# One core, a two-layer hybrid mixer scheduled by its own planner: GpSimd's products and sums may go to VectorE, and the planner counts the SBUF port that the two share

## The chip, the cores and the metric

The kernel runs on one core of a Trainium2 chip. The core has five engines that work side by side, each through its own instructions in order: TensorE (PE; its weight loads are listed apart as PEld), VectorE (DVE), ScalarE (ACT), GpSimd (POOL), and SyncE (SP), which here only issues transfers. An instruction waits at the head of its engine's queue until the semaphores that it names are set, and everything behind it on that engine waits too. The metric is the device time of one execution in microseconds (us); lower is better.

## The reference

Two layers (`DEPTH = 2`) over 256 context tokens and 512 latent tokens of width 1024. One projection `w_in` feeds three branches, which are merged by gates and projected by `w_out`.

```python
def _ssd_chunked(xdt, adt, bm, cm, s0):                 # 32 heads of 64, states of 128
    def body(state, xs):
        xc, ac, bc, cc = xs
        cum = jnp.cumsum(ac, axis=1)
        seg = cum[:, :, None] - cum[:, None, :]
        lmat = jnp.exp(jnp.where(mask, seg, -jnp.inf))
        cb = jnp.einsum('btgn,bsgn->btsg', cc, bc)
        y = jnp.einsum('btsgh,bsghp->btghp', cb[..., None] * lmat, xc)
        y = y + jnp.einsum('btgn,bghnp->btghp', cc, state) * jnp.exp(cum)[..., None]
        dec = jnp.exp(cum[:, -1:] - cum)
        state = state * jnp.exp(cum[:, -1])[..., None, None] \
            + jnp.einsum('bsgn,bsghp->bghnp', bc, xc * dec[..., None])
        return state, y
...
def _lru_gates(xa, wr, br, wi, bi, lam):
    ...
    a = jnp.exp(log_a)
    b = jnp.sqrt(-jnp.expm1(2.0 * log_a)) * (i * xa).astype(jnp.float32)
    return a, b                                         # then h_t = a_t h_{t-1} + b_t
...
def _finish(s, ya, yb, yc, xs, p):
    pa = (ya * jax.nn.silu(s[1])) @ p['w_pa']           # recurrence (LRU)
    ob = _rmsnorm(yb, p['gla_norm_g']).reshape(bn, length, GLA_DV) * jax.nn.silu(s[5])
    pb = ob @ p['w_pb']                                 # gated linear attention (GLA)
    ...
    pc = oc.reshape(bn, length, SSD_INNER) @ p['w_pc']  # state-space branch (SSD)
    g = jax.nn.sigmoid(s[10]).reshape(bn, length, N_BRANCH, D_MODEL)
    merged = g[:, :, 0] * pa + g[:, :, 1] * pb + g[:, :, 2] * pc
    return merged @ p['w_out']
```

All three branches run in both directions. The context's last states start the latent scans.

## The kernel before

Everything is fp32. A product with weights is made of three matmuls of split operands: a weight tile `raw` of 128x1024 arrives by DMA, half of it at a time is cast to `wh` (on ACT or DVE, L328 or L329), and DVE subtracts to get the rest, `wl` (L343). PE then adds `wh` by high input, `wh` by low input and `wl` by high input into a PSUM tile `pp`. The four buffers of `wh` and of `wl` come free as PE finishes with them.

A layer runs in stages. In the **SSD stage** (four groups of two quarters) PE works through weight matmuls while short chains of other work are woven in, in PSUM tiles `aux`:
- the state chain, `ssd_update`: `xw` = `xt` times a decay (POOL), cast to `xwh` (ACT or DVE), remainder `xwl` (DVE or POOL), three matmuls with `btok`, then `sb` or `sf` (the backward and forward states) = old state times decay (POOL) plus the PSUM result (DVE);
- the mask chain, `ssd_ms`: `rr` from DRAM, biases on ACT, a predicated copy with `mlt` (DVE, L388), exp (ACT), times `cb` (POOL, 128x512), a predicated copy with `kd` (DVE), then eight matmuls `aux<-rr,xt`;
- the outputs, `ssd_scan`: `ec` = PSUM times `ec` (DVE), the sum of its two halves (POOL), plus PSUM (DVE), then `gz` times `ec` (DVE); at a group's end `ssd_finish` sums four squares `r<-r,r` (POOL), normalises, and splits `gz` into `oh` and `ol`.

The **GLA stage** follows, then the **LRU stage** (eight blocks: `lru_rec` squares `av` into `w` on POOL, 128x768, and DVE takes `w` times `th`, two gates and three scans), then the output stage.

A planner written in Python, `Sched.loop`, sets the order of all of it while the program is built. Many streams of work are open at once; each shows its next operation. The planner knows a cost for each (`vcost`, `acost`, `gcost`), when each engine and each tile comes free by these costs, and takes the operation that can start first. An operation with more than one way (`any_op`) takes the engine on which it would end first. `copy`, `affine` and `sub` have two ways; `tt`, which makes nearly all of POOL's products and sums, has one, named by its `pool` argument. The result is a fixed order for each engine. What the costs miss shows on the chip as waits.

Of the kernel before, what the change touches and what calls it, by code (L numbers as in the profile page):

```python
# [14 lines left out]
PSUM = bass.MemoryType.PSUM  # L15
# [53 lines left out]
class Cell:  # L69
# [3 lines left out]
    def __init__(self, w=0.0):  # L73
        self.w, self.we, self.r, self.re, self.slots = w, None, 0.0, None, None
# [66 lines left out]
class Sched:  # L141
# [6 lines left out]
    def __init__(self):  # L148
        self.streams = []
        self.done = set()  # L150
        self.cells = {}
        self.eng_free = {"PE": 0.0, "DVE": 0.0, "ACT": 0.0, "POOL": 0.0, "SP": 0.0}
        self.dma_free = 0.0
        self.warm_up = HAM_WINDOW
        self.act_set = None
        self.seq = 0
        self.now = 0.0
# [26 lines left out]
                r = c.r + slack  # L184
        return r

    def op(self, eng, outs, ins, cost, emit):
        yield from self.any_op([(eng, cost, emit)], outs, ins)

    def any_op(self, ways, outs, ins):  # L190

        outs = [self.cell(o) for o in outs]
        ins = [self.cell(i) for i in ins if i is not None and not isinstance(i, (int, float))]
        yield ("op", ways, outs, ins)
        eng, cost, emit = ways[self.way]
        start = self.start_of(eng, outs, ins)
        if eng == "PE":
            if start - self.eng_free[eng] > HAM_WINDOW:
                self.warm_up = HAM_WINDOW
            if self.warm_up > 0:  # L200
                cost *= 2
                self.warm_up -= cost
        extra = emit()
        if isinstance(extra, int):
            cost += extra
        if eng == "SP":
            self.eng_free[eng] = start + 470
            self.dma_free = max(start, self.dma_free) + cost
            fin = self.dma_free + 3000
        else:  # L210
            fin = self.eng_free[eng] = start + cost
        self.now = max(self.now, start)
        for c in outs:
            if fin > c.w:
                c.w, c.we = fin, eng
        for c in ins:
            if fin > c.r:
                c.r, c.re = fin, eng
# [23 lines left out]
    def loop(self):  # L242
        while self.streams:
            best = None
            for s in list(self.streams):
                while s in self.streams:
                    c = s.cur
                    if c is None or (c[0] == "need" and all(n in self.done for n in c[1])) \
                            or (c[0] == "slots" and len(c[1].free) >= c[2]):
                        self.advance(s)  # L250
                        continue
                    break
                else:
                    continue
                if c[0] == "op":
                    for w, (eng, cost, _) in enumerate(c[1]):
                        t = self.start_of(eng, c[2], c[3], LAT + SLACK[eng])
                        if w == 0 or t + cost < t0 + c0:
                            t0, c0, w0 = t, cost, w
                    k = (t0, 0 if s.urgent and s.urgent() else s.prio, s.seq)  # L260
                    if best is None or k < best[0]:
                        best = (k, s, w0)
            if best is None:
                if not self.streams:
                    break
                if any(s.cur is None or (s.cur[0] == "need" and all(n in self.done for n in s.cur[1]))
                       or (s.cur[0] == "slots" and len(s.cur[1].free) >= s.cur[2]) for s in self.streams):
                    continue
                raise RuntimeError("stuck: " + "; ".join(
                    f"{s.key} {s.cur[1] if s.cur[0] == 'need' else s.cur[1].tag}" for s in self.streams))  # L270
            self.way = best[2]
            self.advance(best[1])


class Mixer(Sched):
# [79 lines left out]
        return (0.52 if fast and x.space != PSUM else 1.04) * n + 69  # L355

    def tt(self, out, a, b, op, pool=False):
        eng = self.nc.gpsimd if pool else self.nc.vector
        cost = self.gcost(out.free_size()) if pool else self.vcost(out.free_size(), a)
        yield from self.op("POOL" if pool else "DVE", [out], [a, b], cost, lambda: eng.tensor_tensor(out, a, b, op))  # L360

    def stt(self, out, a, s, b, op0, op1):
        yield from self.op("DVE", [out], [a, s, b], self.vcost(out.free_size(), a) + 60 * (not isinstance(s, float)),
                           lambda: self.nc.vector.scalar_tensor_tensor(out, a, s, b, op0, op1))  # L364

    def ts(self, out, a, s1, s2, op0, op1=None, pool=False):
        eng = self.nc.gpsimd if pool else self.nc.vector
        cost = self.gcost(out.free_size()) if pool else \
            self.vcost(out.free_size(), a, True) + 60 * sum(not isinstance(s, float) for s in (s1, s2) if s is not None)

        def emit():
            if op1 is None:
                eng.tensor_scalar(out, a, s1, s2, op0)
            else:
                eng.tensor_scalar(out, a, s1, s2, op0, op1)
        yield from self.op("POOL" if pool else "DVE", [out], [a, s1, s2], cost, emit)

    def vcopy(self, out, in_):
        yield from self.op("DVE", [out], [in_], self.vcost(out.free_size(), in_, True),
                           lambda: self.nc.vector.tensor_copy(out, in_))  # L380

    def scan(self, out, a, b, init):
        yield from self.op("DVE", [out], [a, b, init], self.vcost(out.free_size(), a),
# [1453 lines left out]
class Layer:  # L1837
# [9 lines left out]
    def open_c(self):  # L1847
# [5 lines left out]
        self.st_o, op = k.pool("oc", "left")  # L1853
        self.acc = [op.tile([P, T], F32, tag=f"acc{j}", name=k.nm("acc")) for j in range(8)]
        self.oh_ = Slots(k, op, "oh", 4, [P, T], F32R)
        self.ol_ = Slots(k, op, "ol", 4, [P, T], F32R)
        self.st_c, c = k.pool("ssd", "right")
# [134 lines left out]
```

## Time and profile before

| | |
|---|---|
| median of 3 runs | 2778.53 us (2775.16 to 2779.71) |
| the profiled execution | 2773.14 us, of which its span is 2771.4 us |
| TensorE clock, mean granted share | 0.993 |
| busy: PE, DVE, ACT, POOL | 2674.1, 2090.7, 1189.4, 583.5 us |
| matmuls; instructions of DVE, POOL | 16294; 3800, 658 |

Busy time is the union of an engine's instructions; it includes what an instruction spends held up once it has begun. An engine's idle time is put down to whatever ended it.

### The profile page before, as it was taken

To read this page: it belongs to the slowest core of one execution; us is meant where nothing else is said; L and a number is where in the kernel's file an instruction comes from. 1 tells how busy PE (TensorE), PEld (TensorE's weight loads), DVE (VectorE), ACT (ScalarE), POOL (GpSimd) and SP (SyncE) were. 2 spreads that over 40 slices of the span, in tenths; PEclk is the share of its full clock that TensorE was granted. 3 is DMA by queue.
4 is the path that set the end of the run, shared out by engine and by line. 5 is a ranking of instruction groups with operands and counts; after the bars stand their busy time and mean duration, and the time that the engine had idled before them with its cause. 6 is when DMAs were issued, how large, how long until landed. Compare 5 with 4: busy or idle time off the path is not lost.

```text
span 2771.4 us, 43082 instructions
## 1 busy us (share of the span) xinstructions
PE 2674.1 (96%) x16294; PEld 2296.3 (83%) x16294; DVE 2090.7 (75%) x3800; ACT 1189.4 (43%) x2278; POOL 583.5 (21%) x658
## 2 busy tenths in 40 slices
PE   7999899999999999999999999999999999999998
PEld 5888788888888888888889887787878888888777
DVE  5778879797665654668956888989897766568987
ACT  5345445353413331325622554555544332245732
POOL 1143425343100000001100215444352000001100
PEclk9999999999999999999999999999999999999999
DMA  6354334434452222552255545344444532243255
GB/s 212 82 146 102 108 101 109 127 89 123 121 179 70 68 74 77 158 179 58 61 166 196 168 103 134 99 107 129 104 115 125 167 84 77 77 150 102 57 157 196
DMA packets 491968, 329.38 MB, mean 119 GB/s; under 512 B 19813, under 2 KB 466865, under 8 KB 491761
## 3 DMA queue, kind: packets, MB, share of 16 engines
q1 hardware_dynamic: 491760, 326.63, 41.8%
q8 instruction: 128, 2.10, 0.3%
q14 instruction: 80, 0.65, 0.1%
HBM read 294.12 MB, written 32.45 MB: 118 GB/s over the span
## 4 chain that ended last, share of the span: by engine, by line
PE 66%; DVE 23%; issue 4%; DMA 3%; ACT 2%; POOL 1%; SPq 0%; DVEq 0%; POOLq 0%; ACTq 0%
PE pp L394 54%; PE aux L394 9%; DVE wl L343 4%; DVE r L364 2%; DMA rr<-cumd 2%; PE aux L398 1%; DVE wh L329 1%; PE aux L403 1%; DVE rr L388 1%; DVE xa L364 1%; DVE gz L364 1%; DMA ada<-in_ada_w_dram 1%; DVE xwl L343 1%; PE aux L535 1%; DMA raw<-in_w_in_dram 1%
## 5 line engine op out<-in xcount | busy, mean ns | idle before, releaser
L394 PE MATMUL pp<-hh,wh 128*128 128x256 f32 (+2 forms) x2624 | 760.1, 351 | 11.0 <-DVE xa L364 6.3
L394 PE MATMUL pp<-hl,wh 128*128 128x256 f32 (+2 forms) x2624 | 765.0, 353 | 0.2 <-DVE hl L343 0.2
L394 PE MATMUL pp<-hh,wl 128*128 128x256 f32 (+2 forms) x2624 | 760.3, 351 | 0.6 <-DVE wl L343 0.6
L394 PEld LDWEIGHTS pp<-hh,wh 128*128 128x128 f32 (+1 forms) x2624 | 486.2, 188 | 72.6 <-issue 7.4
L394 PEld LDWEIGHTS pp<-hh,wl 128*128 128x128 f32 (+1 forms) x2624 | 487.2, 188 | 61.0 <-DVE wl L343 1.4
L394 PEld LDWEIGHTS pp<-hl,wh 128*128 128x128 f32 (+1 forms) x2624 | 486.5, 188 | 61.7 <-issue 2.5
L343 DVE TENSOR_TENSOR wl<-raw,wh 128x512 fp32r<-128x512 f32 (+1 forms) x628 | 470.5, 753 | 42.9 <-ACT wh L328 16.9
L329 DVE CAST wh<-raw 128x512 fp32r<-128x512 f32 (+1 forms) x396 | 186.4, 471 | 315.6 <-PE pp L394 305.9
L319 ACT ACTIVATE rr<-rr,tokp 128x128 f32<-128x128 f32 x640 | 200.6, 390 | 175.6 <-DMA rr<-cumd 175.1
L328 ACT CAST wh<-raw 128x512 fp32r<-128x512 f32 (+1 forms) x232 | 142.0, 617 | 275.1 <-PE pp L394 242.5
L360 POOL TENSOR_TENSOR xw<-xt,tokp 128x256 f32<-128x256 f32 x160 | 134.4, 840 | 199.4 <-ACT xt L328 103.0
L319 ACT ACTIVATE r<-pp 128x768 f32<-128x768 f32 (+1 forms) x112 | 78.4, 700 | 187.8 <-PE pp L394 177.4
L717 POOL TENSOR_SCALAR ss<-ss 128x1 f32<-128x1 f32 x52 | 14.1, 271 | 687.0 <-ACT ob L319 654.6
L360 POOL TENSOR_TENSOR rr<-rr,cb 128x512 f32<-128x512 f32 x80 | 112.3, 1403 | 153.4 <-ACT rr L319 152.8
L360 POOL TENSOR_TENSOR w<-av 128x768 f32<-128x768 f32 x32 | 54.1, 1690 | 419.8 <-ACT av L319 340.5
L394 PE MATMUL pp<-oh,wh 128*128 128x512 f32 (+1 forms) x384 | 119.0, 363 | 2.7 <-DVE gz L364 2.7
L394 PE MATMUL pp<-yh,wh 128*128 128x512 f32 (+1 forms) x384 | 116.9, 358 | 1.3 <-DVE r L364 1.3
L394 PE MATMUL pp<-ol,wh 128*128 128x512 f32 (+1 forms) x384 | 117.4, 359 | 0.1
L394 PE MATMUL pp<-oh,wl 128*128 128x512 f32 (+1 forms) x384 | 117.3, 358 | 0.0
L394 PE MATMUL pp<-yh,wl 128*128 128x512 f32 (+1 forms) x384 | 116.9, 358 | 0.0
L394 PE MATMUL pp<-yl,wh 128*128 128x512 f32 (+1 forms) x384 | 115.8, 356 | 0.0
L394 PE MATMUL pp<-wh,hl 128*128 128x256 f32 x384 | 108.9, 284 | 0.0
(269 smaller groups left out, 5228.8 us busy)
## 6 DMA issues: line engine op xcount, KB each, us to landing
raw<-in_w_in_dram SPq DMA_DIRECT2D x208, 512.0 KB
rr<-cumd SPq DMA_DIRECT2D x160, 256.0 KB
ec<-ecumd SPq DMA_DIRECT2D x160, 128.0 KB
raw<-in_w_out_dram SPq DMA_DIRECT2D x40, 512.0 KB
raw<-in_w_pc_dram SPq DMA_DIRECT2D x32, 512.0 KB
raw<-in_ada_w_dram SPq DMA_DIRECT2D x32, 512.0 KB
ada<-in_ada_w_dram SPq DMA_DIRECT2D x8, 1024.0 KB
raw<-in_w_pb_dram SPq DMA_DIRECT2D x16, 512.0 KB
```

What stands on the lines that cost most here:

```text
L319: self.nc.scalar.activation(out, in_, func, **kw)
L328: yield from self.any_op([("ACT", self.acost(n, in_), lambda: self.nc.scalar.copy(out, in_)), ("DVE", self.vcost(n, in_, True), lambda: se ...
L329: ("DVE", self.vcost(n, in_, True), lambda: self.nc.vector.tensor_copy(out, in_))],
L343: ways = [("DVE", self.vcost(n, a), lambda: self.nc.vector.tensor_tensor(out, a, b, ALU.subtract))]
L360: yield from self.op("POOL" if pool else "DVE", [out], [a, b], cost, lambda: eng.tensor_tensor(out, a, b, op))
L364: lambda: self.nc.vector.scalar_tensor_tensor(out, a, s, b, op0, op1))
L388: lambda: self.nc.vector.copy_predicated(out, mask, data))
L394: lambda: self.nc.tensor.matmul(out, lhsT, rhs, start=start, stop=stop))
L398: yield from self.op("PE", [out], [lhsT, rhs], 2 * rhs.free_size() / 2.4, lambda: self.nc.tensor.matmul(out, lhsT, rhs, start=True, stop=T ...
L403: yield from self.op("PE", [out], [in_, idn], 108, lambda: self.nc.tensor.transpose(out, in_, idn))
L535: yield from self.op("PE", [ps], [self.scf, w], w.free_size() / 2.4, lambda: self.nc.tensor.matmul(out, lt, w, start=k < 4, stop=k >= 4, t ...
L717: yield from self.op("POOL", [r], [ss], 150, lambda: self.nc.gpsimd.tensor_scalar(r, ss, 1.0 / width, EPS, ALU.mult, ALU.add))
```

## The change

`tt` with `pool=True` now offers both DVE and POOL, and the planner picks. The planner also keeps the last five stretches in which DVE and POOL used the port that it takes them to share: a POOL operation, or a DVE operation none of whose operands lies in PSUM (for `stt`, `ts`, `vcopy` and operations with several ways), is costed longer by its overlap with the other engine's stretches. Scans and predicated copies are not counted. Where an operation has several ways, the longer cost also enters the choice.

```diff
+        self.port = {"DVE": [], "POOL": []}
...
+    def shared(self, eng, start, cost):
+
+        for a, b in self.port["POOL" if eng == "DVE" else "DVE"]:
+            cost += max(0.0, min(b, start + cost) - max(a, start))
+        return cost
+
+    def any_op(self, ways, outs, ins, port=True):
+
+        port = port and all(x.space != PSUM for x in outs + ins if x is not None and not isinstance(x, (int, float)))
...
+        if eng == "POOL" or (eng == "DVE" and port):
+            cost = self.shared(eng, start, cost)
+            self.port[eng] = self.port[eng][-5:] + [(start, start + cost)]
...
                     for w, (eng, cost, _) in enumerate(c[1]):
                         t = self.start_of(eng, c[2], c[3], LAT + SLACK[eng])
+                        if len(c[1]) > 1 and (eng == "POOL" or (eng == "DVE" and c[4])):
+                            cost = self.shared(eng, t, cost)
...
     def tt(self, out, a, b, op, pool=False):
-        eng = self.nc.gpsimd if pool else self.nc.vector
-        cost = self.gcost(out.free_size()) if pool else self.vcost(out.free_size(), a)
-        yield from self.op("POOL" if pool else "DVE", [out], [a, b], cost, lambda: eng.tensor_tensor(out, a, b, op))
+
+        n = out.free_size()
+        ways = [("DVE", self.vcost(n, a), lambda: self.nc.vector.tensor_tensor(out, a, b, op))]
+        if pool:
+            ways.append(("POOL", self.gcost(n), lambda: self.nc.gpsimd.tensor_tensor(out, a, b, op)))
+        yield from self.any_op(ways, [out], [a, b])
```

How many instructions stand on which engine in the two programs:

| instruction | POOL before | POOL now |
|---|---|---|
| `rr` times `cb`, 128x512 | 80 | 9 |
| `sb`, `sf` times decay, 128x256 | 64, 64 | 8, 7 |
| `ec` sum, 128x256 | 64 | 9 |
| `w` = `av` squared, 128x768 | 32 | 3 |
| `r<-r,r`, 128x768 and 128x512 | 12, 12 | 6, 6 |
| `hl` (split of the layer's input) | 10 | 5 |
| `xw`, 128x256 | 160 | 157 |
| `xwl`, 128x256 | 20 | 48 |

Of the casts that may go to either, 32 of `wh` and 23 of `xwh` moved from DVE to ACT. All engines' orders differ in most places, since the planner's times differ.

First place: DVE in the SSD stage of the first layer, fourth group, between the first and the second predicated copy of one mask (`rr_6481` before, `rr_6521` now). Before:

```order
L343 TENSOR_TENSOR wl_6412<-raw_6178,wh_6411 128x512
L343 TENSOR_TENSOR ol_6423<-gz_4851,oh_6422 128x768
L364 SCALAR_TENSOR_TENSOR r_6414<-r_6475,r_6414 128x768
L360 TENSOR_TENSOR sb_6433<-sb_6433,aux_6477 128x256
L388 COPY_PREDICATED rr_6481<-mlt,rr_6483 128x512
L343 TENSOR_TENSOR xwl_6531<-xw_6522,xwh_6530 128x256
L343 TENSOR_TENSOR wl_6497<-raw_6304,wh_6496 128x512
L364 SCALAR_TENSOR_TENSOR gz_5014<-gz_5014,p_63_226,r_6174 128x768
L343 TENSOR_TENSOR wl_6545<-raw_6304,wh_6544 128x512
L364 SCALAR_TENSOR_TENSOR gz_6540<-r_6541,pp_6413 128x768
L360 TENSOR_TENSOR sb_6524<-sb_6524,aux_6536 128x256
L388 COPY_PREDICATED rr_6481<-ident,kd_6328 128x512
```

Now:

```order
L404 COPY_PREDICATED rr_6521<-mlt,rr_6523 128x512
L342 CAST wh_6584<-raw_6318 128x512
L356 TENSOR_TENSOR wl_6585<-raw_6318,wh_6584 128x512
L380 SCALAR_TENSOR_TENSOR gz_6587<-r_6588,pp_6432 128x768
L342 COPY xt_6426<-aux_6576 128x2x128
L373 TENSOR_TENSOR rr_6521<-rr_6521,cb_6288 128x512
L356 TENSOR_TENSOR xwl_6612<-xw_6600,xwh_6611 128x256
L404 COPY_PREDICATED rr_6521<-ident,kd_6344 128x512
L342 CAST wh_6644<-raw_6458 128x512
L356 TENSOR_TENSOR wl_6645<-raw_6458,wh_6644 128x512
L373 TENSOR_TENSOR sf_6602<-sf_6602,aux_6626 128x256
L373 TENSOR_TENSOR sf_6661<-sf_6602,etr_725 128x256
```

The product with `cb` and the state's product with `etr` now stand in DVE's own row, the first between the two predicated copies, with an `xwl` right behind it.

Second place: POOL, the same group. Before:

```order
L360 TENSOR_TENSOR xw_6375<-xt_5901,tokp_711 128x256
L360 TENSOR_TENSOR sb_6377<-sb_6276,etr_712 128x256
L360 TENSOR_TENSOR xw_6431<-xt_5901,tokp_711 128x256
L360 TENSOR_TENSOR sb_6433<-sb_6377,etr_712 128x256
L360 TENSOR_TENSOR rr_6347<-rr_6347,cb_6250 128x512
L345 TENSOR_TENSOR xwl_6443<-xw_6431,xwh_6442 128x256
L360 TENSOR_TENSOR xw_6522<-xt_5901,tokp_711 128x256
L360 TENSOR_TENSOR sb_6524<-sb_6433,etr_712 128x256
L360 TENSOR_TENSOR rr_6481<-rr_6481,cb_6250 128x512
L360 TENSOR_TENSOR xw_6582<-xt_5901,tokp_711 128x256
```

Now:

```order
L375 TENSOR_TENSOR xw_6400<-xt_6051,tokp_724 128x256
L375 TENSOR_TENSOR xw_6447<-xt_6051,tokp_724 128x256
L358 TENSOR_TENSOR xwl_6453<-xw_6447,xwh_6452 128x256
L375 TENSOR_TENSOR rr_6359<-rr_6359,cb_6288 128x512
L375 TENSOR_TENSOR xw_6502<-xt_6051,tokp_724 128x256
L375 TENSOR_TENSOR xw_6545<-xt_6051,tokp_724 128x256
L375 TENSOR_TENSOR xw_6600<-xt_6051,tokp_724 128x256
```

POOL's queue is nearly the `xw` of the state chain alone; the products that stood between one `xw` and the next are gone from it.

Third place: DVE in the LRU stage of the first layer, the fourth block. Before:

```order
L343 TENSOR_TENSOR wl_13187<-raw_13020,wh_13186 128x512
L364 SCALAR_TENSOR_TENSOR w_2336_13182<-w_2336_13182,th_13065 128x768
L364 SCALAR_TENSOR_TENSOR th_13123<-th_13123,xa_13014 128x768
L343 TENSOR_TENSOR wl_13219<-raw_13020,wh_13218 128x512
L364 SCALAR_TENSOR_TENSOR xa_13221<-pp_13101,p_61_224,xa_13221 128x8x63
```

Now:

```order
L373 TENSOR_TENSOR w_2338_13186<-av_13187 128x768
L380 SCALAR_TENSOR_TENSOR w_2338_13186<-w_2338_13186,th_13086 128x768
L380 SCALAR_TENSOR_TENSOR th_13127<-th_13127,xa_13016 128x768
L373 TENSOR_TENSOR w_2338_13186<-av_13215 128x768
L380 SCALAR_TENSOR_TENSOR w_2338_13186<-w_2338_13186,th_13147 128x768
L380 SCALAR_TENSOR_TENSOR xa_13225<-pp_13091,p_61_224,xa_13225 128x8x63
```

Two squares of `av` have come into DVE's row, and both `w` steps stand ahead of the next block's convolution `xa`.

## Rows read from the trace of the kernel before

**Rows 1.** The page, parts 1 and 4: busy time by engine; chain by engine.

```profile
PE 2674.1 (96%) x16294; PEld 2296.3 (83%) x16294; DVE 2090.7 (75%) x3800; ACT 1189.4 (43%) x2278; POOL 583.5 (21%) x658
...
PE 66%; DVE 23%; issue 4%; DMA 3%; ACT 2%; POOL 1%; SPq 0%; DVEq 0%; POOLq 0%; ACTq 0%
```

**Rows 2.** Busy time by stretch: SSD, LRU of each layer (from:to, length, engines).

```profile
100.00:735.00 635.00, 614.69 (x3856) 526.32 (x3856) 516.67 (x917) 301.41 (x678) 235.72 (x242) 0.99 0.43 111
...
1130.00:1425.00 295.00, 290.12 (x1777) 252.11 (x1776) 230.17 (x331) 138.67 (x184) 27.31 (x18) 1.00 0.41 119
...
1590.00:2135.00 545.00, 523.71 (x2959) 429.80 (x2959) 480.69 (x859) 274.97 (x592) 218.44 (x236) 1.00 0.44 114
...
2440.00:2772.00 332.00, 310.32 (x1644) 268.70 (x1642) 273.40 (x405) 159.44 (x237) 32.81 (x24) 0.98 0.43 132
```

**Rows 3.** PE's waits in 100:735: us in total, times, longest.

```profile
PE aux L394 <- ACT xwh L328: 4.3, 4, 2.0
PE aux L394 <- DVE xwh L329: 3.9, 3, 1.8
PE aux L394 <- DVE xwl L343: 3.5, 6, 1.3
```

**Rows 4.** PE's waits in 1590:2135.

```profile
PE aux L394 <- DVE xwh L329: 5.2, 5, 1.7
...
PE aux L394 <- DVE xwl L343: 2.7, 6, 0.6
```

**Rows 5.** Timelines of DVE and POOL, 415:432: start, length, instruction.

```profile
418.12 2.31 DVE L343 TENSOR_TENSOR wl<-raw,wh 128x512 fp32r<-128x512 f32 x1
420.35 1.89 DVE L329 CAST xwh<-xw 128x256 fp32r<-128x256 f32 x1
...
418.03 4.06 POOL L360 TENSOR_TENSOR r<-r,r 128x768 f32<-128x768 f32 x2
```

**Rows 6.** Groups by shape, POOL: count, busy us, mean ns, idle before.

```profile
L360 POOL TENSOR_TENSOR xw<-xt,tokp 128x256 f32<-128x256 f32 x160 | 134.4, 840 | 199.4 <-ACT xt L328 103.0 <-DVE xwl L343 80.8 <-DVE xt L329 13.6
L360 POOL TENSOR_TENSOR rr<-rr,cb 128x512 f32<-128x512 f32 x80 | 112.3, 1403 | 153.4 <-ACT rr L319 152.8
L360 POOL TENSOR_TENSOR sb<-sb,etr 128x256 f32<-128x256 f32 x64 | 55.5, 867 | 96.3 <-DVE sb L360 73.3 <-PE aux L394 13.4 <-ACT sb L328 6.9
L360 POOL TENSOR_TENSOR w<-av 128x768 f32<-128x768 f32 x32 | 54.1, 1690 | 419.8 <-ACT av L319 340.5 <-DVE wl L343 20.1 <-DVE g L364 19.8
L360 POOL TENSOR_TENSOR ec<-ec 128x256 f32<-128x256 f32 x64 | 50.6, 791 | 119.3 <-DVE ec L360 118.8
L360 POOL TENSOR_TENSOR sf<-sf,etr 128x256 f32<-128x256 f32 x64 | 48.6, 760 | 131.8 <-PE aux L394 81.9 <-DVE sf L360 15.4 <-ACT sf L328 15.1
```

**Rows 7.** Groups by shape, DVE.

```profile
L343 DVE TENSOR_TENSOR wl<-raw,wh 128x512 fp32r<-128x512 f32 x624 | 468.5, 754 | 42.9 <-ACT wh L328 16.9 <-PE pp L394 1.5
L329 DVE CAST wh<-raw 128x512 fp32r<-128x512 f32 x395 | 186.0, 471 | 315.6 <-PE pp L394 305.9 <-DMA raw<-in_w_in_dram 4.2 <-DMA raw<-in_w_pa_dram 2.9
L343 DVE TENSOR_TENSOR xwl<-xw,xwh 128x256 fp32r<-128x256 f32 x140 | 77.4, 553 | 4.4 <-ACT xwh L328 2.2
```

**Rows 8.** Single tiles on DVE: ns shortest/median/longest, first and last start.

```profile
L343 DVE TENSOR_TENSOR wl<-raw,wh x628: 544/691/2316, 40.5 to 2757.2; 128x512 fp32r<-128x512 f32 x156, 128x384 fp32r<-128x384 f32 x1
L329 DVE CAST wh<-raw x396: 353/426/1687, 40.2 to 2755.4; 128x512 fp32r<-128x512 f32 x197, 128x384 fp32r<-128x384 f32 x1
L343 DVE TENSOR_TENSOR xwl<-xw,xwh x140: 401/425/1523, 119.2 to 2090.4; 128x256 fp32r<-128x256 f32 x140
L364 DVE SCALAR_TENSOR_TENSOR th<-th,xa x32: 943/952/2222, 1163.2 to 2654.4; 128x768 f32<-128x768 f32 x32
L360 DVE TENSOR_TENSOR ec<-ec,aux x80: 395/414/423, 142.5 to 2112.6; 128x256 f32<-128x256 f32 x80
```

**Rows 9.** DVE's waits over the whole run.

```profile
DVE rr L388 <- ACT rr L319: 24.6, 26, 2.1
...
DVE rr L388 <- POOL rr L360: 11.6, 10, 2.1
```

More of the change, by code (lines that the diff above doesn't have):

```diff
@@ L185, in start_of, with op @@
         return r
-    def op(self, eng, outs, ins, cost, emit):
-        yield from self.any_op([(eng, cost, emit)], outs, ins)
-    def any_op(self, ways, outs, ins):
+    def op(self, eng, outs, ins, cost, emit, port=False):
+        yield from self.any_op([(eng, cost, emit)], outs, ins, port)
+    def shared(self, eng, start, cost):
[4 more added lines that the diff above has]
+        port = port and all(x.space != PSUM for x in outs + ins if x is not None and not isinstance(x, (int, float)))
         outs = [self.cell(o) for o in outs]
         ins = [self.cell(i) for i in ins if i is not None and not isinstance(i, (int, float))]
-        yield ("op", ways, outs, ins)
+        yield ("op", ways, outs, ins, port)
         eng, cost, emit = ways[self.way]
@@ L357, in tt @@
     def tt(self, out, a, b, op, pool=False):
-        eng = self.nc.gpsimd if pool else self.nc.vector
-        cost = self.gcost(out.free_size()) if pool else self.vcost(out.free_size(), a)
-        yield from self.op("POOL" if pool else "DVE", [out], [a, b], cost, lambda: eng.tensor_tensor(out, a, b, op))
+        n = out.free_size()
[3 more added lines that the diff above has]
+        yield from self.any_op(ways, [out], [a, b])
     def stt(self, out, a, s, b, op0, op1):
         yield from self.op("DVE", [out], [a, s, b], self.vcost(out.free_size(), a) + 60 * (not isinstance(s, float)),
-                           lambda: self.nc.vector.scalar_tensor_tensor(out, a, s, b, op0, op1))
+                           lambda: self.nc.vector.scalar_tensor_tensor(out, a, s, b, op0, op1), True)
     def ts(self, out, a, s1, s2, op0, op1=None, pool=False):
@@ L375, in emit @@
                 eng.tensor_scalar(out, a, s1, s2, op0, op1)
-        yield from self.op("POOL" if pool else "DVE", [out], [a, s1, s2], cost, emit)
+        yield from self.op("POOL" if pool else "DVE", [out], [a, s1, s2], cost, emit, True)
     def vcopy(self, out, in_):
         yield from self.op("DVE", [out], [in_], self.vcost(out.free_size(), in_, True),
-                           lambda: self.nc.vector.tensor_copy(out, in_))
+                           lambda: self.nc.vector.tensor_copy(out, in_), True)
     def scan(self, out, a, b, init):
```

## The prediction

> **What bounds the kernel now.** Start with the page. PE is busy for 96% of the span, DVE for 75%, POOL for 21%; the chain that ended last is PE for 66% and DVE for 23% [rows 1]. So POOL itself is nowhere the bound, and a change of engines can only move what PE waits for. The table by stretch tells where that is: in the two SSD stretches PE stands idle for 635 - 614.69 = 20.3 and 545 - 523.71 = 21.3 us, 41.6 in all, while DVE is busy for 81% and 88% of them and POOL does 454 of its 583.5 us [rows 1, 2]. In the first LRU stretch PE is idle for 4.9 us, in the last stretch for 21.7 (its LRU and output stage and the end of the program) [rows 2]. The waits of PE in the SSD stretches name the state chain: `xwh` and `xwl` end 4.3 + 3.9 + 3.5 + 5.2 + 2.7 = 19.6 us of the 41.6 [rows 3, 4]. These waits are few and short, 24 of up to 2.0 us: PE is late only where DVE has a queue.
>
> Then look at what makes DVE late. At 418 us a `wl` took 2.31 us and the `xwh` behind it 1.89, while POOL ran two `r<-r,r` in one stretch of 4.06 [rows 5]. The same `wl` takes 0.691 in the middle of its group [rows 8]. So an SBUF instruction of DVE is held up by one of POOL. With an operand in PSUM it is not: `ec<-ec,aux` took between 395 and 423 ns in all 80 cases [rows 8].
>
> **The change, part by part.** Moved to DVE, by the table of counts: 71 products `rr`, 56 + 57 + 55 of 128x256 (`sb`, `sf`, `ec`), 29 `w`, 12 `r`, 8 others. DVE did none of these, so I price each by DVE's median for two SBUF operands of its width: 0.425 for 256 (`xwl`), 0.691 for 512 (`wl`), 0.952 for 768 (`th`) [rows 8]. That is 71 x 0.691 + 168 x 0.425 + 29 x 0.952 + 6 x 0.952 + 6 x 0.691 + 8 x 0.425 = 49.1 + 71.4 + 27.6 + 9.9 + 3.4 = 161 us more. Moved off: 28 `xwl` x 0.425, 32 `wh` x 0.426 and 23 `xwh` at half a `wh`, 0.21: 30 us less. The casts go to ACT, busy for 43% [rows 1]; that costs nothing while ACT has such gaps, and some 0.4 us each, by DVE's row, if it has none. Net, DVE gets 131 us.
>
> Against this stands what DVE wins back at the port. Mean less median, times count, is (754 - 691) x 624 = 39 us for `wl`, (471 - 426) x 395 = 18 for `wh` and (553 - 425) x 140 = 18 for `xwl` [rows 7, 8]: 75 us lost in three kinds. Some of the other SBUF kinds lose too: the longest `th` took 2.222 for a median of 0.952 [rows 8]. The moved products make up 71/80 x 112.3 + 56/64 x 55.5 + 57/64 x 48.6 + 55/64 x 50.6 + 29/32 x 54.1 = 284 us of POOL's busy time [rows 6]; the other moves (`r` and `hl` off, `xwl` on) nearly cancel. So about half of POOL's time goes. Half of 75 is 38, which leaves the other kinds out; twice as much is the most that I would read from these rows. I take 60. DVE's own time then grows by some 70 us, 20 of it in the LRU stages (27.6 for `w`, less about 7 of port) and 50 in the SSD stretches.
>
> What of that reaches PE? DVE has 1180 - 997 = 183 us idle in the SSD stretches [rows 2], and PE's 41.6 us of idle time there stand against 997 us of DVE's work, 4%. At that rate 50 us cost 2 us, and in the LRU stages 20 us cost 1. The bounds are nothing, if all falls into DVE's idle time, and the whole 70 us, if all falls where DVE has a queue and PE is next. The low rate is nearer to the rows, since a 96% busy PE mostly has weight matmuls to go on with.
>
> The gain is in the state chain. POOL's queue keeps the `xw`, and loses the `rr` (mean 1.40), `sb` (0.87) and `sf` (0.76) between them [rows 6]; DVE's `xwh` and `xwl`, next in the chain, meet half as much of POOL's port time. The `rr` chain loses a hop, and 1.40 becomes about 0.69. And the planner now counts overlaps such as those at 418 us, so that it should put PE's `aux` matmuls behind more weight matmuls where DVE is late. The bounds are nothing and the 41.6 us; the nearest rows are the 19.6 us of `xwh` and `xwl`, of which I take 12, about the share of POOL's work that leaves the chain's neighbourhood with a little for the order. GLA keeps its instructions but for a few copies: nothing.
>
> In the LRU stages each block now has two squares in DVE's row ahead of `xa`, 1.9 us, where before a `w` on POOL could hold a `th` up for 2.222 - 0.952 = 1.3 [rows 8]. That is the 1 us above; its upper bound is the 20 us.
>
> [...] By the rows, the 75 us of three kinds stand against POOL's 583.5 busy us [rows 1]: a small part of POOL's time falls on DVE. [...]
>
> Sum against the profiled execution: 2773.1 - 12 + 3 = 2764. The median of the runs shown is 5.4 us above that execution, so on the median 2778.5 - 9 = 2769.5; I write 2769. A measurement of this kernel tells about 0.2%, 5.5 us, from no change: below 2773 is faster, above 2784 slower.
>
> **The rivals.**
> *A trade without effect*: what the port gives back on DVE and what the products cost it cancel where PE waits, and the weaving of the chains stays as good as it was. For it: PE is 96% busy, and the 19.6 us are spread over 24 waits. Against it: the 2 us stall behind the 4.06 us of POOL is not a matter of sums. 2778, within 5 us. Chance 0.24.
>
> *The wait takes POOL's place on DVE*: slower. POOL stood idle for 152.8 us before its `rr` because ACT's exp was not ready, and nothing was behind it but POOL's own work [rows 6]. Now 71 of these products stand in DVE's row, with `xwl` behind them. Their price: DVE's first predicated copy waits for ACT's `rr` for 24.6 us over 80 cases, 0.31 each; 71 x 0.31 = 22 us, less 71/80 of the 11.6 us that the second copy waited for POOL, 12 us of DVE idle [rows 9]. With the 50 us of added work, DVE's row is 62 us longer in the SSD stretches. If a third of that comes where PE's next matmul needs it, PE loses 21 us, and the 12 us do not come, since it is the same chain: 2778.5 + 21 = 2799. It cancels the gain when a fifth of the 62 us reaches PE, and makes the kernel measurably slower from 12 + 5.5 of 62 us, 28%. Against it: the planner places the product only when it believes exp to be done, and the present rate is 4%. Chance 0.24.
>
> *The big gain*: if DVE nearly always has an SBUF instruction next, POOL's products cost it their full length, and 284 - 131 = 153 us come free on DVE. Two thirds of the SSD stretches' 41.6 us would go: 2778.5 - 28 = 2750. Against it: 75 us is all that three of the largest kinds lose now. Chance 0.12.
>
> That the change does nothing is excluded by the table of counts.
>
> **How the numbers follow.** The forecast, a small gain between 2759 and 2773, has 0.40. Faster than 2773 is the forecast and the big gain, 0.52; same 0.24; slower 0.24. The range goes down to 2740, past the big gain's 2750 and near the loss of all 41.6 us, and up to 2800, which takes in the slower rival's own sum and about half of what it may give: about 0.03 lie below it and 0.12 above. The likeliest case's own range is 2759 to 2773.
>
> **What the profile of the changed kernel would show.** Right: POOL busy near 300 us; `wl`'s mean on DVE nearer to 691, `xwl`'s nearer to 425; `xw`'s mean on POOL lower; DVE busy at 2130 to 2190; PE's idle time in the SSD stretches near 30 us, with less of it ended by `xwh` and `xwl`. Wrong: the DVE instructions `rr` (the product) and `sb` or `sf` with idle time ended by ACT or PE, above some 20 us; PE waits ended by `xh` or `xa` grown by more than a few us in the LRU stages; or PE's waits as large as before, moved to other tiles. What would make the forecast wrong above all is that the two orders differ nearly everywhere, so that each of the 24 small waits is drawn anew.

## The result, and the profile after

The changed kernel takes 2755.14 us (median of 4 runs, 2754.36 to 2756.88) against 2779.12 (4 runs, 2775.16 to 2782.96): a ratio of 0.9915, 95% interval 0.9897 to 0.9932. It is 24 us faster, where 9.5 were forecast. The profiled execution of after took 2755.44 us, near its own median; that of before, 2773.14, was 6 us below its median, so the two traces differ by only 17.8 us of span, and only these can be looked for in them.

The page of after, span and part 1 (busy time by engine), beside [rows 1]:

```profile
span 2753.6 us, 42894 instructions
PE 2667.7 (97%) x16294; PEld 2298.6 (83%) x16294; DVE 2104.9 (76%) x3990; ACT 1222.8 (44%) x2350; POOL 297.5 (11%) x398
```

POOL is down to the 300 us that were named as a sign; DVE has 190 instructions more and is busy for only 14 us more, not 40 to 100.

Busy time by stretch, cut at the same places of the program as [rows 2] (from:to, length, then PE, PEld, DVE, ACT, POOL, granted clock, DMA share, GB/s):

```profile
100.00:731.80 631.80, 613.31 (x3864) 528.28 (x3863) 536.82 (x1006) 326.21 (x722) 117.08 (x130) 0.98 0.43 112
...
1126.90:1424.00 297.10, 289.00 (x1767) 251.97 (x1766) 232.14 (x344) 138.13 (x186) 0.74 (x2) 0.99 0.40 115
...
1586.80:2126.00 539.20, 526.83 (x2949) 432.45 (x2949) 486.05 (x946) 284.51 (x615) 107.70 (x124) 0.99 0.45 116
...
2428.40:2754.00 325.60, 306.88 (x1644) 267.78 (x1642) 270.97 (x412) 162.44 (x243) 9.54 (x11) 0.99 0.44 135
```

The SSD stretches are 3.2 and 5.8 us shorter, and PE is idle in them for 18.5 + 12.4 = 30.9 us, from 41.6. The first LRU stretch is 2.1 us longer; the last stretch, for which a small loss was forecast, 6.4 shorter.

PE's waits in the first SSD stretch (us in total, times, longest), beside [rows 3]:

```profile
PE aux L414 <- DVE rr L404: 12.6, 7, 5.4
PE pp L410 <- DVE r L380: 2.7, 1, 2.7
PE aux L410 <- DVE xwh L342: 1.0, 1, 1.0
PE aux L410 <- ACT xwh L341: 0.7, 2, 0.5
PE aux L410 <- DVE xwl L356: 0.5, 2, 0.3
```

And in the second, beside [rows 4]:

```profile
PE aux L410 <- ACT xwh L341: 3.4, 4, 1.4
...
PE aux L414 <- DVE rr L404: 1.2, 3, 0.6
...
PE aux L410 <- DVE xwl L356: 0.9, 3, 0.6
PE aux L410 <- DVE xwh L342: 0.6, 2, 0.5
```

The waits for `xwh` and `xwl`, 19.6 us before, are 1.0 + 0.7 + 0.5 + 3.4 + 0.9 + 0.6 = 7.1 now. One wait came in their place: that for the mask `rr`, 13.8 us in the two stretches. Over the whole of before it was less than half of that:

```profile
PE aux L398 <- DVE rr L388: 5.7, 10, 1.9
```

So 8.1 of the 12.5 us came back at the mask, and the two kinds of wait together fell by 4.4. Of the other 6.3 us of PE's idle time that went (41.6 to 30.9), 5.3 lie in waits for `ct` and `gz`. Before, the first line from the first SSD stretch, the others from the second:

```profile
PE pp L394 <- DVE ct L364: 2.9, 1, 2.9
...
PE pp L394 <- DVE gz L364: 2.7, 2, 2.0
...
PE aux L403 <- DVE ct L360: 1.4, 1, 1.4
```

After, both from the second:

```profile
PE aux L419 <- DVE ct L373: 1.1, 1, 1.1
...
PE pp L410 <- DVE gz L380: 0.8, 2, 0.5
```

The longest wait for the mask, 5.4 us, ends at 298.6 us. Within it, with PE idle, TensorE's granted clock falls from 1.00 (293 to 294 us) to 0.50 (295 to 296 us), and over 295 to 310 us it is 0.50 on average (columns as above):

```profile
295.00:310.00 15.00, 6.57 (x32) 5.05 (x32) 14.76 (x26) 5.99 (x14) 1.34 (x2) 0.50 0.50 136
```

DVE's groups by shape (count, busy us, mean ns, idle before them), beside [rows 7]:

```profile
L356 DVE TENSOR_TENSOR wl<-raw,wh 128x512 fp32r<-128x512 f32 x624 | 440.6, 709 | 46.9 <-ACT wh L341 14.7 <-PE pp L410 8.0 <-PE aux L410 0.5
L342 DVE CAST wh<-raw 128x512 fp32r<-128x512 f32 x363 | 159.0, 438 | 300.4 <-PE pp L410 282.6 <-DMA raw<-in_w_in_dram 12.0 <-DMA raw<-in_w_pa_dram 2.7
L373 DVE TENSOR_TENSOR rr<-rr,cb 128x512 f32<-128x512 f32 x71 | 52.4, 739 | 3.8 <-ACT rr L332 3.3
L356 DVE TENSOR_TENSOR xwl<-xw,xwh 128x256 fp32r<-128x256 f32 x112 | 47.1, 421 | 5.2 <-ACT xwh L341 3.9
L380 DVE SCALAR_TENSOR_TENSOR th<-th,xa 128x768 f32<-128x768 f32 x32 | 30.5, 952 | 0.0
L373 DVE TENSOR_TENSOR w<-av 128x768 f32<-128x768 f32 x29 | 27.6, 953 | 6.7 <-ACT av L332 6.7
L373 DVE TENSOR_TENSOR sf<-sf,etr 128x256 f32<-128x256 f32 x57 | 25.6, 450 | 17.2 <-PE aux L410 16.1
L373 DVE TENSOR_TENSOR sb<-sb,etr 128x256 f32<-128x256 f32 x56 | 25.3, 452 | 2.0 <-ACT sb L341 0.3
L373 DVE TENSOR_TENSOR ec<-ec 128x256 f32<-128x256 f32 x55 | 23.5, 427 | 1.5
```

The five moved groups cost 154.4 us, close to their prices. The means of the three kinds that the prediction reads fell: `wl` 754 to 709, `wh` 471 to 438, `xwl` 553 to 421. The product `rr` waited for ACT for only 3.3 us, not 22: the planner does put it where exp is done. Before `sf`'s product DVE stood idle for 16.1 us until PE was done, under the 20 named as a sign of being wrong. Two groups of POOL, beside [rows 6]:

```profile
L375 POOL TENSOR_TENSOR xw<-xt,tokp 128x256 f32<-128x256 f32 x157 | 133.5, 850 | 529.3 <-DVE xwl L356 349.5 <-ACT xt L341 171.6 <-PE aux L419 2.6
L358 POOL TENSOR_TENSOR xwl<-xw,xwh 128x256 fp32r<-128x256 f32 x48 | 40.6, 845 | 160.7 <-ACT xwh L341 148.8 <-PE pp L410 8.7 <-DVE xwh L342 3.1
```

`xw` is not shorter (850 ns, 840 before), though a lower mean was named as a sign. Its single cases show more than the mean (ns shortest/median/longest, before and then after):

```profile
L360 POOL TENSOR_TENSOR xw<-xt,tokp x160: 607/666/3477, 105.2 to 2085.3; 128x256 f32<-128x256 f32 x160
...
L375 POOL TENSOR_TENSOR xw<-xt,tokp x157: 608/929/2983, 106.4 to 2074.0; 128x256 f32<-128x256 f32 x157
```

The shortest is as it was, the median went from 666 to 929 ns. POOL too is held up by DVE, whose instructions with two operands in SBUF became more, not fewer: 84 of the 157 `xw` took over 800 ns, and during each of these such an instruction ran on DVE, a `wl` during 40 of them and during 16 of the other 73. The 25 `xw` that met none took 731 ns at most.

### The profile page after: what moved, and what is told of

Read it like the earlier page. It is cut to its first block, busy times and chain, and to the rows that moved or that the text cites. A ratio compares the mean times of both kernels' runs of the same rounds, so it can differ in the third digit from the quotient of the medians.

```text
span 2753.6 us, 42894 instructions
## 1 busy us (share of the span) xinstructions
PE 2667.7 (97%) x16294; PEld 2298.6 (83%) x16294; DVE 2104.9 (76%) x3990; ACT 1222.8 (44%) x2350; POOL 297.5 (11%) x398
## 5 line engine op out<-in xcount | busy, mean ns | idle before, releaser
L356 DVE TENSOR_TENSOR wl<-raw,wh 128x512 fp32r<-128x512 f32 (+1 forms) x628 | 442.6, 708 | 46.9 <-ACT wh L341 14.7
L342 DVE CAST wh<-raw 128x512 fp32r<-128x512 f32 (+1 forms) x364 | 159.4, 438 | 300.4 <-PE pp L410 282.6
L341 ACT CAST wh<-raw 128x512 fp32r<-128x512 f32 (+1 forms) x264 | 161.8, 617 | 233.2 <-PE pp L410 195.2
L410 PE MATMUL pp<-wl,hh 128*128 128x256 f32 x384 | 108.7, 283 | 0.0
L410 PE MATMUL pp<-wh,hh 128*128 128x256 f32 x384 | 108.7, 283 | 0.0
```

The costliest lines, as they stand in the source:

```text
L341: yield from self.any_op([("ACT", self.acost(n, in_), lambda: self.nc.scalar.copy(out, in_)), ("DVE", self.vcost(n, in_, True), lambda: se ...
L342: ("DVE", self.vcost(n, in_, True), lambda: self.nc.vector.tensor_copy(out, in_))],
L356: ways = [("DVE", self.vcost(n, a), lambda: self.nc.vector.tensor_tensor(out, a, b, ALU.subtract))]
L410: lambda: self.nc.tensor.matmul(out, lhsT, rhs, start=start, stop=stop))
```

## The experiments

Three theories stand against each other. The move (A): products leave POOL, which holds DVE up less, and the state chain is shorter. The planner's counting of the port (B), which could gain without any move. And a draw (C): the two orders differ nearly everywhere, and the new one may only be luckier. One run is an edit of the kernel before, all others are edits of the changed kernel; each was timed in 5 rounds beside the kernel before, which stood at 2777.7 to 2778.5 us.

**The move without the counting.** The planner no longer lengthens a step for the port that it takes the two engines to share.

```diff
         for a, b in self.port["POOL" if eng == "DVE" else "DVE"]:
-            cost += max(0.0, min(b, start + cost) - max(a, start))
+            pass
```

> The products may go to either engine, but the planner costs no overlap at the port (POOL keeps 17 sb, 11 sf, 15 rr, 3 w and 6 ec products, and takes 91 xwl instead of 20). Theory A, the gain is the move itself (shorter chains, less of POOL's port time): 2758 to 2766, two thirds or more of the 24 us. Theory B, the gain is the planner's truer costs: 2772 to 2782. Theory C, the gain is one lucky draw among many orders: anywhere between 2750 and 2785.

Measured: 2752.78 us, ratio 0.991 (0.9895 to 0.9925). The whole gain is there. POOL is busy for 350.1 us in it, DVE for 2116.4.

**The counting without the move.** `tt` goes by its flag again, and its cost is counted at the port.

```diff
     def tt(self, out, a, b, op, pool=False):
...
-        if pool:
-            ways.append(("POOL", self.gcost(n), lambda: self.nc.gpsimd.tensor_tensor(out, a, b, op)))
-        yield from self.any_op(ways, [out], [a, b])
+        eng = self.nc.gpsimd if pool else self.nc.vector
...
+        yield from self.op("POOL" if pool else "DVE", [out], [a, b], cost, lambda: eng.tensor_tensor(out, a, b, op), True)
```

> POOL keeps all its products as before; only the planner's costs count the shared port. Theory A: 2772 to 2782, little gain, since POOL's products and their port time stay. Theory B: 2755 to 2764, most of the gain, since the order now knows of the overlaps that held up wl and xwh. Theory C: anywhere between 2750 and 2785.

Measured: 2768.84 us, ratio 0.9969 (0.9958 to 0.998). The order that counting alone gives is 9 us faster than before; with the move, counting shows no gain of its own (2755.14 with it, 2752.78 without). That is one order each, so 9 us is not far beyond what a mere redraw does (below).

**Two more draws.** The latency that the planner puts between engines, 200, is 220: in the kernel before and in the changed one.

```diff
-LAT = 200
+LAT = 220
```

> The kernel before, with the planner's delay from engine to engine set to 220 instead of 200: a redraw of the order with nothing else changed. Theories A and B: within 6 us of 2779. Theory C: off by 10 us or more, to either side.

> The changed kernel with the same redraw of the order (delay 220 instead of 200). Theories A and B: within 6 us of 2755, so that it stays some 20 us ahead of the kernel before. Theory C: 2765 to 2785, the gain mostly gone.

Measured: before 2784.63 us, ratio 1.0023 (1.0013 to 1.0034); after 2759.86, ratio 0.9937 (0.9921 to 0.9952). Another order moves either kernel by 5 to 7 us, and the two stay 25 us apart. One redraw of each is few, but the other runs point the same way: four orders with the SSD products on POOL (before, its redraw, counting alone, `w` alone free) took 2766 to 2785 us, five in which the planner is free to place them took 2744 to 2760. Luck is an unlikely explanation of 24 us, though it may be one of 5.

**POOL reads again, in the same order.** With each product that `tt` puts on DVE, POOL does as many products of 128x256 on a spare tile that nothing reads, 430 in all. PE, DVE, ACT and SP have the instructions of after, in its order. The second run has twice as many memsets in their place, which write SBUF and read nothing.

```diff
+        def on_dve():
+            self.nc.vector.tensor_tensor(out, a, b, op)
+            if pool:
...
+                for _ in range(n // 256):
+                    self.nc.gpsimd.tensor_tensor(self.spare, one, one, ALU.mult)
...
-        ways = [("DVE", self.vcost(n, a), lambda: self.nc.vector.tensor_tensor(out, a, b, op))]
+        ways = [("DVE", self.vcost(n, a), on_dve)]
```

> The changed kernel with its order kept on PE, DVE, ACT and SP, row by row; for each product that went to DVE, POOL also does products of 128x256 on a spare tile that nobody reads (427 of them, some 270 us of POOL's time, much like what the change took off it). If the gain is POOL's time at the port and in front of xw: DVE's wl and xwl grow longer again and the time goes back to 2766 to 2779. If the gain is the shorter chains and DVE's own order (no hop to POOL and back): 2754 to 2759.

> As the run with spare products, but POOL fills the spare tile with zeros instead (854 memsets of 128x256, which read no SBUF). If what counts is that POOL reads SBUF while DVE has two SBUF inputs: 2754 to 2759. If POOL's mere occupation in front of xw counts, or any write of POOL holds DVE up: like the run with products, 2766 to 2779.

Measured: with products 2800.99 us, ratio 1.0081 (1.0068 to 1.0094); with memsets 2751.12, ratio 0.9909 (0.9892 to 0.9925). The page (part 1) of the run with products:

```profile
PE 2677.5 (96%) x16294; PEld 2298.5 (82%) x16294; DVE 2187.9 (78%) x3990; ACT 1223.2 (44%) x2350; POOL 650.2 (23%) x828
```

And of the run with memsets:

```profile
PE 2666.0 (97%) x16294; PEld 2297.4 (84%) x16294; DVE 2110.1 (77%) x3990; ACT 1223.0 (44%) x2350; POOL 557.9 (20%) x1258
```

Groups by shape of DVE and POOL with the products:

```profile
L356 DVE TENSOR_TENSOR wl<-raw,wh 128x512 fp32r<-128x512 f32 x624 | 461.5, 743 | 45.0 <-ACT wh L341 12.7 <-PE pp L418 7.4 <-PE aux L418 0.5
...
L375 DVE TENSOR_TENSOR gz<-gz,ec 128x128 f32<-128x128 f32 x160 | 58.7, 405 | 1.4
...
L379 POOL TENSOR_TENSOR spare<-ones 128x256 f32<-128x256 f32 x430 | 359.6, 836 | 20.5
```

And with the memsets:

```profile
L356 DVE TENSOR_TENSOR wl<-raw,wh 128x512 fp32r<-128x512 f32 x624 | 442.6, 712 | 47.5 <-ACT wh L341 14.7 <-PE pp L418 8.0 <-PE aux L418 0.5
...
L375 DVE TENSOR_TENSOR gz<-gz,ec 128x128 f32<-128x128 f32 x160 | 45.6, 323 | 1.4
...
L379 POOL MEMSET spare<- 128x256 f32 x860 | 276.0, 321 | 39.7
```

PE's longest sum of waits in the run with products:

```profile
PE aux L422 <- DVE rr L412: 27.7, 24, 6.1
```

This is the clearest pair of the study. POOL's 353 us of reading hold DVE up for 83 us with not one DVE instruction more (2104.9 to 2187.9), and the kernel loses 46 us, more than was expected: half of what DVE lost. POOL's 276 us of writing cost nothing. So what costs is not that POOL works, and not its queue, but its reads, and these the change took away. DVE's busy time grew by 83.0 us with the reads and by 5.2 with the writes.

The shorter chains stand in both runs. With them, and with POOL busy for 650.2 us (583.5 before), the kernel with the products is still 23 us slower than before (2777.87 beside it). So the chains do not make the gain by themselves in this order, which was planned without the added reads.

**Only one stage's products.** First the SSD products go back to POOL, all with an edit like that of `rr`, and only `w` in the LRU stages is free; then the reverse, with the edit of `w` alone.

```diff
+        if pool == "only":
+            ways = ways[1:]
...
-            yield from self.tt(m, m, S.cb[g][:, c, :].unsqueeze(1).to_broadcast([P, 4, P]), ALU.mult, True)
+            yield from self.tt(m, m, S.cb[g][:, c, :].unsqueeze(1).to_broadcast([P, 4, P]), ALU.mult, "only")
```

```diff
-            yield from self.tt(w2[:, d], av, av, ALU.mult, True)
+            yield from self.tt(w2[:, d], av, av, ALU.mult, "only")
```

> The port is counted, w in the LRU stages may go to DVE, and the products and sums of the SSD stages (rr, sb, sf, ec, r) stay on POOL. Planner's counting alone gave 2769. If the SSD products make the gain: 2765 to 2773, about that. If the LRU squares make it: 2754 to 2762.

> The change, but w in the LRU stages stays on POOL (32 products of 128x768). With only w moved the time was 2766, with nothing moved and the port counted 2769. If POOL's port time is what costs: w held up th and hf, so 2757 to 2764, a little behind the change. If the LRU stages gain nothing from the move: 2752 to 2757.

Measured: `w` free alone 2765.7 us, ratio 0.9958 (0.9944 to 0.9971), 3 us from the counting alone; the SSD products free alone 2749.44, ratio 0.9896 (0.9882 to 0.9909), 6 us below after and below both ranges that were written down. The gain is that of the SSD products; for `w` these runs show none clear of a draw (3 us faster beside the counting alone, 6 slower beside the SSD products alone).

**Further in the same direction.** POOL gets no product of `tt` at all; then it keeps `xw` alone, and every `xwl` goes to DVE too.

```diff
-        if pool:
-            ways.append(("POOL", self.gcost(n), lambda: self.nc.gpsimd.tensor_tensor(out, a, b, op)))
```

```diff
-        if pool:
-            ways.append(("POOL", self.gcost(n), lambda: self.nc.gpsimd.tensor_tensor(out, a, b, op)))
+        if pool == "only":
+            ways = [("POOL", self.gcost(n), lambda: self.nc.gpsimd.tensor_tensor(out, a, b, op))]
...
-        yield from self.sub(wl, xw, wh.bitcast(F32), True)
+        yield from self.sub(wl, xw, wh.bitcast(F32))
```

> Every product and sum of tt on DVE, xw too (160 more of 128x256); POOL keeps only 23 xwl, 4 hl and the normalisations. If POOL's port time is what costs: a little better than the change, 2745 to 2755, since DVE gives up some 68 us and wins back some 60. If DVE's load is what costs once the port is free: 2760 to 2775.

> All of tt's products on DVE but xw, which POOL does, all 160, and xwl all on DVE: POOL keeps one product in each step of the state chain. The run with xw on DVE too took 2806. If xw's place is what made that run slow (its DVE row holds xw, xwh and xwl one behind the other, and the weight casts with them): 2748 to 2760. If it is DVE's load as such, of which xw is only a third: 2765 to 2790.

Measured: no product on POOL 2805.69 us, ratio 1.0102 (1.0087 to 1.0118), slower than before, where a gain or a small loss against after was expected; `xw` alone on POOL 2778.16, ratio 1.0001 (0.9992 to 1.0011), in the range named for DVE's load as such. The page, a group of DVE and then two of PE's waits, in the first of them:

```profile
PE 2681.6 (96%) x16294; PEld 2314.9 (83%) x16294; DVE 2162.5 (77%) x4292; ACT 1195.6 (43%) x2274; POOL 90.2 (3%) x168
```

```profile
L356 DVE TENSOR_TENSOR wl<-raw,wh 128x512 fp32r<-128x512 f32 x624 | 428.7, 690 | 47.0 <-ACT wh L341 14.7 <-PE pp L408 8.1 <-DVE wh L342 0.5
```

```profile
PE aux L412 <- DVE rr L402: 28.8, 11, 7.2
PE aux L408 <- DVE xwh L342: 20.6, 9, 2.6
```

On average DVE's instructions are hardly held up any more (`wl` at 690 ns, the 691 of the undisturbed median of [rows 8]), and yet PE waits for the mask for 28.8 us and for `xwh` for 20.6. This is the rival in which the wait takes POOL's place on DVE, one step further on: the products that POOL did beside DVE now stand in the one row from which PE is fed.

TensorE's clock was lower there too. The mean granted share is 0.980 in the first of these two runs and 0.985 in the second, against 0.991 in after and in the run with POOL's products. In the first, PE is idle for most of 289 to 303 us (busy for 3.58 + 1.71 of 14), and the clock is 0.76 in 289 to 296 us and 0.50 from there to 330:

```profile
289.00:296.00 7.00, 3.58 (x18) 2.82 (x19) 5.84 (x14) 0.67 (x2) 0.00 (x0) 0.76 0.60 151
296.00:303.00 7.00, 1.71 (x6) 0.93 (x4) 3.10 (x8) 6.79 (x14) 0.00 (x0) 0.50 0.18 42
303.00:330.00 27.00, 13.72 (x60) 10.52 (x60) 26.53 (x54) 14.32 (x36) 0.73 (x1) 0.50 0.31 87
```

PE is busy for 13.9 us more than in after with the same 16294 matmuls (13.8 in the second run). How much of that is the clock is not separated: with POOL's products, at 0.991, PE is busy for 9.8 us more too.

**Casts off DVE.** A cast or copy that either engine can do goes to DVE only where that is 300 ns earlier; in the second run, on top of `xw` alone on POOL.

```diff
-                        if w == 0 or t + cost < t0 + c0:
+                        margin = 300 if eng == "DVE" else 0
+                        if w == 0 or t + cost + margin < t0 + c0:
```

> The change, but a cast or copy goes to DVE only if it would end 0.3 us earlier there than on ACT: 263 of the 364 wh casts and 11 xwh that DVE had now go to ACT, some 115 us off DVE and 165 onto ACT, which was busy for 44%. In the run with spare products 83 us more on DVE cost 46. If DVE's load reaches PE at about that rate both ways: 2700 to 2735. If DVE's load costs only where a port wait or a late xwh stands in a burst: 2745 to 2757. If ACT's own waits (for rr's transfers) then hold the weights up: above 2757.

> Both of the last two edits: only xw on POOL, casts on ACT unless DVE is 0.3 us earlier. If both help on their own: the best of all, 2695 to 2735. If DVE's load is not what PE waits for: within 6 us of the run with only xw on POOL.

Measured: 2744.03 us, ratio 0.9877 (0.9863 to 0.9891), the fastest version found, 11 us below after, and 2764.73, ratio 0.9949 (0.9937 to 0.9961). The page of the first:

```profile
PE 2667.0 (97%) x16294; PEld 2299.2 (84%) x16294; DVE 1988.7 (72%) x3690; ACT 1380.3 (50%) x2658; POOL 286.1 (10%) x388
```

DVE has 116 us less to do than in after, and the kernel gains 11 of them: the time is just below the range named for a load that costs only in places (2745 to 2757), and above the 2700 to 2735 of a rate of one half. The second run, with DVE at 2005.3 us, has 100 less than after and is 10 us slower; against `xw` alone on POOL it gains 13, which is neither of its two ranges. DVE's total alone does not set the time; which of its instructions are late does.

**Where each run differs.** The stages can be cut at two events that every trace has in both layers: the first `aux<-v,ket` matmul (GLA begins) and ACT's first `xa<-pp,p` (LRU begins). In after they are the first starts in these rows of the tiles' timelines:

```profile
L410 PE MATMUL aux<-v,ket x80: 377/379/382, 828.8 to 1110.5; 128*128 128x256 f32 x80
...
L332 ACT ACTIVATE xa<-pp,p x8: 975/988/993, 1140.5 to 1363.0; 128x768 f32<-128x768 f32 x8
...
L410 PE MATMUL aux<-v,ket x80: 377/379/380, 2188.7 to 2411.0; 128*128 128x256 f32 x80
...
L332 ACT ACTIVATE xa<-pp,p x3: 992/994/994, 2434.4 to 2509.0; 128x768 f32<-128x768 f32 x3
```

The differences of such starts, in us of each profiled execution:

| run | start and SSD | GLA | LRU, output, second SSD | GLA | LRU to the end |
|---|---|---|---|---|---|
| before | 832.0 | 311.5 | 1054.3 | 248.1 | 325.5 |
| after | 828.8 | 311.7 | 1048.2 | 245.7 | 319.2 |
| move, no counting | 818.7 | 311.6 | 1054.7 | 248.2 | 319.5 |
| counting, no move | 829.2 | 311.2 | 1055.2 | 245.7 | 326.1 |
| before, 220 | 848.0 | 311.3 | 1055.1 | 246.1 | 324.3 |
| after, 220 | 834.7 | 311.1 | 1042.9 | 244.8 | 325.1 |
| POOL reads | 845.2 | 311.6 | 1071.6 | 246.2 | 322.1 |
| POOL writes | 828.5 | 311.6 | 1042.9 | 246.2 | 320.5 |
| only `w` free | 828.4 | 311.5 | 1058.7 | 245.7 | 319.3 |
| only SSD free | 826.2 | 311.5 | 1038.5 | 245.6 | 324.0 |
| all on DVE | 851.9 | 311.4 | 1073.2 | 245.8 | 322.1 |
| `xw` on POOL | 841.6 | 311.3 | 1058.2 | 245.6 | 323.7 |
| casts to ACT | 819.1 | 312.2 | 1044.8 | 245.5 | 323.0 |
| both of these | 835.9 | 311.2 | 1046.6 | 245.2 | 324.0 |

The first GLA stage takes 311.1 to 312.2 us in all of them. What differs stands nearly all in the two columns with SSD: all on DVE is 23 and 25 us behind after there, POOL's reads 16 and 23. The columns also show how a draw looks: after and the move without counting end within 1 us of one another, and one is 10 us ahead in the first column, 6.5 behind in the third. Not all of such a difference is the order: the run with POOL's writes has after's order on PE, DVE and ACT and is 5.3 us shorter in the third column.

## Why the prediction was right, and where its sizes were off

**The place and the state chain.** Right. The waits for `xwh` and `xwl` fell by 12.5 us (12 were taken), PE's idle time in the SSD stretches to 30.9 (near 30), the SSD stretches by 9.0 (12 less 2). That the last two sizes agree is in part luck: 8.1 of the 12.5 us came back at `rr`, and other waits, for `ct` and `gz` above all, which no step had, fell by 6.3. The pair of runs with POOL's reads and writes shows the cause, POOL's reads, apart from any order (DVE's busy time up by 83.0 us with the reads, by 5.2 with the writes). That a port lies behind it is the planner's assumption, and not shown.

**The products' price on DVE.** Right: the five large groups, 154.4 us, are at the medians they were priced by, a little above for `rr` (739 for 691) and `sf`, `sb` (450 for 425).

**What DVE wins back: mis-sized.** Taken as 60 us, with DVE growing by 70; it grew by 14. Mean before less mean after, times the smaller count, gives 28 us for `wl`, 15 for `xwl` and 12 for `wh`, 55 in the three kinds where 38 of their 75 were counted; all kinds but these three give 38 where 22 were counted, `th`, `xwh` and `gz<-gz,ec` 7 each of it. That makes 93, 33 more than the 60. Of the other 24 us, 11 are the `xwl`, `wh` and `xwh` that left, priced at their undisturbed length (30 us) where their means come to 42; 11 are other copies and casts that left DVE and that the price did not have (`k`, `xt` and `acc` the largest); 8 are neighbours that overlap, which busy time counts once; and the instructions moved in cost 6 more than their price. The rows to read would have been every group's mean against its median, not three. The big gain's premise, POOL's whole length credited to DVE, is shown by no run: 93 us back for 284 us of POOL's work is a third, and POOL's added reads cost DVE 83 us for 353, a quarter. The time itself, 2755, lies outside the likeliest case's own range (2759 to 2773) and nearer to that rival's 2750 than to my 2769, but it did not come by that rival's road: DVE has no 153 us free.

**The rate at which DVE's time reaches PE: mis-sized.** The 4% was PE's idle time over DVE's work, an average. The run with POOL's reads puts a marginal rate beside it: 83 us of DVE cost 43 us of span, 0.52; all on DVE, 58 us of DVE cost 51, in another order and at a lower clock. In the other direction the rate is small again: 116 us of casts off DVE gave back 11. The waits say where DVE's time counts: at `rr`, `xwh` and `xwl`, behind DVE's queue. That weight matmuls cover such a wait only as far as the planner foresaw it is my reading, and not shown. The forecast survived this since DVE's own time hardly grew; by my own sum, 0.52 of the expected 70 us would have eaten the 12.

**The slower rival.** Not come for its reason (3.3 us of the product's wait for ACT, not 22), but its mechanism exists: PE's wait for `rr` went from 5.7 to 13.8 us, and with all products on DVE to 28.8 and a slower kernel. Of the signs of being wrong, waits that move to other tiles came for 8.1 of the 12.5 us. Among the splits that were run the change stands near the best; it leaves `xw` and part of `xwl` on POOL.

**LRU and the rest.** The 1 us of loss was 2.1 in the first LRU stage. The end of the program gained 6.4 us, which no step had. From ACT's first `xa` it is 319 to 321 us in four runs with `w` on DVE and 324 to 326 in the four with `w` on POOL; but six other runs with `w` mostly or all on DVE have 322 to 325. So `w` may gain there, and what these 6 us are stays open, as do 2.6 in the second GLA stage and 2.2 in the first output stage.

**The sum.** Of the 14.5 us by which the gain exceeded the forecast, 6 lie between before's profiled execution and its median, and the rest in the stages outside SSD, 9 us shorter where 1 longer was forecast; draws of 5 to 7 us can be a part of it. Why the next 85 us of POOL's work (297.5 to 212.5, `xw` alone left) cost as much as the first 286 gained is settled only as far as PE's waits show it; DVE's load, the order and the granted clock (0.985 against 0.991) changed together there.

## What to carry to other kernels

Two engines that hold each other up should be priced by what each costs the other: here a quarter to a third of POOL's reading time fell on DVE, and of the 83 us of it that the added reads cost, half reached the end of the program though PE was 96% busy. That half is no rule: 116 us of casts off DVE were worth 11. Move work off the slow engine until the fast one's queue, not the hold-up, makes the bound engine wait; past that point (`xw` alone left on POOL, then nothing) the gain went back to zero and beyond, with the granted clock falling from 0.991 to 0.985 and 0.980. Before crediting a few us to a cause, draw the order again: unchanged work moved by 5 to 7 us.

## What the hardware showed that I had not expected

In the two runs above POOL's memset of 128x256 took 321 ns on average and its product of the same size 836; 860 of the one left DVE's time as it was (2110.1 against 2104.9) where 430 of the other added 83 us. The hold-up is spread unevenly: in the run with POOL's reads `gz<-gz,ec` of 128x128, which is in the SSD stages alone, went from 314 to 405 ns, `wl` of 128x512, which is in every stage, from 709 to 743.
